# Small triangle products of the first third of the tokens: odd chunks in the other column half of the array, two PSUM tiles instead of one

## The chip, the cores and the metric

The kernel runs on one core of one Trainium2 chip. The metric is device time in microseconds (us) of one execution. A core has five engines that run side by side: TensorE (PE in the profile; PEld is its weight load), VectorE (DVE), ScalarE (ACT), GpSimd (POOL) and SyncE (SP), which here issues nearly all DMA transfers. Each engine works through its own instructions strictly in the order in which they stand, and waits on semaphores for the others.

## The reference

One layer of a bidirectional diffusion backbone over 128 context tokens and 2048 latent tokens, 1024 channels, fp32. All tokens are normalised and modulated, and go through one input projection; half of the channels (8 heads of 64) then run an RWKV-7 recurrence in both directions, the other half a gated short convolution; one output projection and a normalisation end it.

```python
def step(S, inp):
    r_t, w_t, k_t, v_t, kk_t, a_t = inp
    s_kk = jnp.einsum('bdhij,bdhj->bdhi', S, kk_t)
    S = (S * w_t[..., None, :] - s_kk[..., :, None] * (kk_t * a_t)[..., None, :]
         + v_t[..., :, None] * k_t[..., None, :])
    return S, jnp.einsum('bdhij,bdhj->bdhi', S, r_t)
```

The kernel does not step through tokens one by one. It cuts them into 34 chunks of 64. For each chunk, head and direction it needs a 64x64 product of two scaled operands, called alpha and beta below; of these products the triangles by the diagonal and the low off-diagonal block are kept in DRAM (scratch arrays `at` and `lo`), and a later stage solves with them. Those 64x64 products are what the change touches.

## The kernel before, in words

The work is written as a program of tiles; a scheduler then puts the instructions of each engine in an order, by a model of its own of how long each takes, and that order is fixed when the kernel runs. The trace's line numbers are those of the source.

**Stages.** Phase 1 computes the projections, the gates, the convolution and the scaled operands. It goes over the tokens in three thirds (`THIRD`: blocks 0 and 1, 2 and 3, 4 and 5; a block is 384 tokens, six chunks, the last 256). Within a third it goes over four groups `g` of 128 channels (two heads each), and for each group over the two blocks `j` of the third: `mixA` (the operands of the recurrence and the triangle products), `convB`, then `gateA`, `gateB`. Phase 2 solves, carries the states and forms the outputs; phase 3 is the output projection.

**The dense work around.** Each projection is 24 matmuls of 128x128 by 384 columns (L166 to L168; tiles `mmk`, `mmr`, `mmc`, `mmu`, `mmv`, `mmg`, `mmgb`, `mmb`). `lup` adds two matmuls (L420, L421) into a tile `up` of the same pool of five PSUM tiles (`pmm`). A smaller pool, `pax`, has three PSUM tiles with the tag `ax`, used in turn by `part_sum` (L210, L211: tiles `pss`, `psb`, `psq`), by the triangle products (`psA`) and by a transpose (`psv`). Whoever takes the next `ax` tile waits until the last reader of the tile three takings back is done.

**The triangle products.** `mixA` makes, for each direction `d`, the operands (`pair`, VectorE, L443 to L455; the last of them is L455) and calls `triangles`. In the first third (`late` is empty) it calls it once for each direction, 16 calls in all; in the second and third third once for both directions together (`todo` holds two). A call does six chunks times two heads of 64x64 by 64 columns. Head `h` takes the array's row half `h`. `place(d, h)` chooses the column half, and with it the half of the PSUM partitions that the result goes to: direction 0 puts head 0 in the upper and head 1 in the lower half, direction 1 the other way. So a call for one direction uses two of the four 64x64 quarters of the array, and a call for both directions all four, with one PSUM tile for each direction.

**After the products.** ScalarE copies the PSUM tile into the tile `ta` (L382, 128 x 384) and then two strips of 32 partitions over it (L384, two copies of 32 x 192). SyncE stores both halves of `ta` to DRAM: `at` (L385, pieces of 32 numbers) and `lo` (L386, per partition 6 x 32 numbers in a row). `ta` has two buffers; before the products it held an activation (L439), which VectorE reads for L454. So L439 of a later call waits until the stores of an earlier call have landed.

**Other names used below.** `wr` and `w` are weights on their way in (L130 load, L131 and L132 split, L133 store of the split); `wgate`/`psgr` a side product spread over the first third (L196); `t` is L426 (ScalarE's reading of `up`); `ct` L516; `sqx`/`ssq` the norm of the next third's tokens; `ops` the stored operands (L356).

## Time and profile before

| what | value |
|---|---|
| time, median of 3 runs | 1651.73 us (1645.61, 1651.73, 1653.22) |
| profiled execution: span, first to last instruction | 1642.5 us (its own time outside the span is not on the page) |
| mean granted TensorE clock | 0.974 |
| first triangle product | at 97.57 us of the span |
| last of the first third's 16 calls | at 371.08 us |
| first call of the second third | at 424.14 us |

The page names an engine's busy time, then groups of instructions by source line with their count, and for idle time the instruction that ended it. A row of the timeline gives start, duration, engine, line and tile, and in brackets how long the engine had been idle and what released it; successive equal instructions are merged into one row. A matmul of fp32 numbers stands as two records, so twelve 64x64 products are 24 records.

### The profile page before, as it was taken

Reading aid. Unit: us, or ns where it says so; the run is one execution under the profiler, and the core shown is the slowest. Engines: PE = TensorE matmul, PEld = TensorE weight load, DVE = VectorE, ACT = ScalarE, POOL = GpSimd, SP = SyncE. Lnnn points to the kernel's source line nnn. Section 1 sums busy time; section 2 is a strip of 40 time slices with the busy share of each in tenths; the row PEclk is TensorE's granted clock in tenths of the full one; section 3 lists DMA queues with packets and bytes.
Section 4 is the critical chain, followed back from the end, with each engine's and each line's share of the span. In section 5 each row is a group of like instructions: output and inputs, shape, how many; then the busy total and the mean of one; then the engine's idle time right before and its main releaser. Section 6 shows DMA issues by size and latency. Waiting matters only on the chain.

```text
span 1642.5 us, 42385 instructions
## 1 busy us (share of the span) xinstructions
PE 1531.9 (93%) x17160; PEld 1405.2 (86%) x17160; DVE 1104.6 (67%) x2220; ACT 762.7 (46%) x1617; POOL 586.8 (36%) x1040
## 2 busy tenths in 40 slices
PE   5899999999999999999989999989999988789998
PEld 2899988999999999999988898878888876668886
DVE  5876978784738685658788794566776764574333
ACT  4554565554425452425554023757666673432222
POOL 0011211110112021102667474888888832022221
PEclk8899999999999999999999999999999998889999
DMA  9677668664746564656867858767767663264342
GB/s 377 202 272 251 237 222 300 212 230 179 236 156 195 176 210 149 203 182 203 275 203 228 285 173 256 183 166 188 215 169 202 185 160 93 66 199 166 122 151 93
DMA packets 237988, 327.23 MB, mean 199 GB/s; under 512 B 91288, under 2 KB 191896, under 8 KB 223712
## 3 DMA queue, kind: packets, MB, share of 16 engines
q1 hardware_dynamic: 231840, 318.55, 61.3%
q0 software_dynamic: 1200, 3.93, 0.6%
q8 instruction: 135, 2.21, 0.6%
q10 hardware_dynamic: 4752, 2.04, 0.5%
q14 instruction: 61, 0.50, 0.1%
HBM read 207.92 MB, written 116.54 MB: 198 GB/s over the span
## 4 chain that ended last, share of the span: by engine, by line
PE 45%; POOL 9%; DVE 8%; ACT 4%; issue 4%; DMA 3%; SPq 0%; DVEq 0%; POOLq 0%; ACTq 0%
POOL zt L950 4%; PE psu L1381 4%; PE psu L1382 4%; PE psu L1383 4%; POOL ztmp L947 3%; PE psE L840 2%; PE psS L840 2%; ACT fg L829 1%; PE mmc L166 1%; PE mmg L168 1%; PE mmg L166 1%; PE mmg L167 1%; PE mmc L167 1%; PE mmc L168 1%; PE mmv L166 1%
## 5 line engine op out<-in xcount | busy, mean ns | idle before, releaser
L950 POOL TENSOR_TENSOR zt<-zt,ztmp 128x30 f32<-128x30 f32 (+7 forms) x390 | 153.0, 392 | 30.6
L840 PE MATMUL psE<-fg 128*64 128x128 f32 x2176 | 135.4, 277 | 15.8 <-ACT fg L831 13.6
L840 PEld LDWEIGHTS psE<-fg 128*64 128x64 f32 x2176 | 120.6, 139 | 22.4 <-ACT fg L831 15.6
L840 PE MATMUL psS<-sv,E 128*64 128x64 f32 x2176 | 98.6, 233 | 19.0 <-DVE sv L1147 18.5
L840 PEld LDWEIGHTS psS<-sv,E 128*64 128x64 f32 x2176 | 81.6, 143 | 34.8 <-DVE sv L1147 24.9
L329 POOL TENSOR_TENSOR shk<-rawl 128x384 f32<-128x384 f32 (+1 forms) x24 | 23.5, 979 | 241.1 <-ACT rawl L325 221.8
L829 ACT ACTIVATE fg<-psX 64x512 f32<-64x512 f32 x136 | 80.5, 592 | 37.3 <-PE psX L840 35.2
L1448 POOL TENSOR_TENSOR z<-z,x 128x512 f32<-128x512 f32 x32 | 41.8, 1307 | 137.9 <-DVE z L1444 114.4
L947 POOL TENSOR_TENSOR ztmp<-ab,zt 128x60 f32<-128x60 f32 (+4 forms) x165 | 85.9, 521 | 12.9
L1147 DVE TENSOR_TENSOR sv<-psS,pc 64x128 f32<-64x128 f32 x254 | 63.8, 278 | 39.5 <-PE psS L840 37.6
L329 POOL TENSOR_TENSOR shv<-rawl 128x384 f32<-128x384 f32 (+1 forms) x24 | 21.3, 888 | 165.0 <-ACT rawl L325 164.8
L831 ACT COPY fg<-psG 64x256 f32<-64x256 f32 x136 | 49.9, 367 | 52.5 <-DVE fg L1048 29.0
L1048 DVE TENSOR_TENSOR fg<-psG,consts 64x256 f32<-64x256 f32 x136 | 57.4, 422 | 25.1 <-ACT fg L831 11.2
L1041 DVE TENSOR_TENSOR F<-psF,consts 128x512 f32<-128x512 f32 x68 | 44.1, 681 | 44.5 <-PE psF L840 44.5
L446 POOL COPY pcs<-pp 128x6 f32<-128x6 f32 (+1 forms) x48 | 20.9, 435 | 139.0 <-ACT pp L435 135.1
L166 PE MATMUL mmc<-h,w 128*128 128x384 f32 (+1 forms) x192 | 64.6, 336 | 5.9 <-ACT q1r L327 4.1
L1109 DVE TENSOR_TENSOR E<-psE,consts 128x256 f32<-128x256 f32 x136 | 53.2, 418 | 21.3 <-PE psE L840 19.9
L166 PE MATMUL mmg<-h,w 128*128 128x384 f32 (+1 forms) x192 | 63.6, 331 | 3.8 <-ACT q1v L327 3.8
L831 ACT COPY E<-psE 128x256 f32<-128x256 f32 x136 | 48.5, 373 | 36.8 <-DVE E L1109 27.4
L166 PE MATMUL mmb<-h,w 128*128 128x384 f32 (+1 forms) x192 | 63.3, 329 | 1.5 <-ACT ta L439 1.5
L166 PE MATMUL mmgb<-h,w 128*128 128x384 f32 (+1 forms) x192 | 64.0, 333 | 0.4 <-ACT q1r L327 0.4
L166 PE MATMUL mmv<-h,w 128*128 128x384 f32 (+1 forms) x192 | 63.4, 330 | 0.3 <-ACT q1r L327 0.3
(325 smaller groups left out, 5169.9 us busy)
## 6 DMA issues: line engine op xcount, KB each, us to landing
w<-scr_wsp SPq DMA_DIRECT2D x68, 1024.0 KB, 5.7
scr_wsp<-w SPq DMA_DIRECT2D x34, 1024.0 KB, 4.9
scr_ops<-pair SPq DMA_DIRECT2D x80, 384.0 KB, 4.5
wr<-in_win SPq DMA_DIRECT2D x34, 512.0 KB, 6.8
o<-scr_ops SPq DMA_DIRECT2D x32, 512.0 KB, 6.0
fg<-scr_ops SPq DMA_DIRECT2D x120, 128.0 KB, 3.6
x<-in_x SPq DMA_DIRECT2D x17, 512.0 KB, 8.5
wadas<-in_wada SPq DMA_DIRECT2D x8, 1024.0 KB, 13.5
```

Source lines behind the costliest of these rows:

```text
L166: T.matmul(ps[:, :n], w[:, 0, k], hh[:, 0, k, :n], start=k == 0, stop=False)
L829: P.activation(dst, src, AF.Copy, scale=-1.0)
L831: P.copy(dst, src)
L840: r = T.matmul(*a, start=True, stop=True, **k)
L947: eng.tensor_tensor(tv, ab[:, j:j + 2, j + 2:32].unsqueeze(1).broadcast_to((128, kn, 2, n)), zt[:, :kn, j:j + 2].unsqueeze(3).broadcast_to ...
L950: last = eng.tensor_tensor(zt[:, :kn, j + 2:32], zt[:, :kn, j + 2:32], tv[:, :, r], ALU.subtract).ins
L1048: V.tensor_tensor(g.gs[H[1 - h], g.op, h, us], ps[gi][r, :, 64:128], B.mG[r, g.d].unsqueeze(1).broadcast_to((64, 4, 64)), ALU.mult)
L1109: V.tensor_tensor(to(H[1]), of(H[1]), B.mE[:, g.d].unsqueeze(1).broadcast_to((128, 4, 64)), ALU.mult)
L1147: r = V.tensor_tensor(dst, sp[gi][0:64, q], B.pc[0:64, d, 2 * p:2 * p + 2, c:c + 1].broadcast_to((64, 2, 64)), ALU.mult)
L1381: T.matmul(ps[:], mh[:, n], hi[:, cs], start=start and n == 0, stop=False)
L1382: T.matmul(ps[:], mh[:, n], lo[:, cs], start=False, stop=False)
L1383: T.matmul(ps[:], ml[:, n], hi[:, cs], start=False, stop=stop and n == 3)
```

## The change

Only calls with one direction, those of the first third, are changed: `split` is 2 there and 1 elsewhere. A call now takes two PSUM tiles of `pax`, one for even and one for odd chunks. Odd chunks (`k` = 1) use `place(d, 1 - h)`, the other column half, so their result stands with the halves of the partitions swapped. ScalarE copies each tile into the chunks of `ta` that it holds (L388, every second chunk; four strips at L390 instead of two). The stores of the even chunks go out as before but for every second chunk (L392 `at`, L393 `lo`); those of the odd chunks need two DMAs each, one for each half of the partitions, which puts the halves back in place (L397 `at`, L398 `lo`). So a call has 2 + 4 copies instead of 1 + 2, and 6 stores instead of 2; every stored row is now in pieces of 32 numbers.

```diff
-        ps = [pax.tile([128, 6, 64], F32, tag="ax", name=f"psA{g}_{j}_{x[0]}") for x in todo]
+        split = 3 - len(todo)
+        m = nch // split
+        ps = [[pax.tile([128, 6 // split, 64], F32, tag="ax", name=f"psA{g}_{j}_{x[0]}_{k}") for k in range(split)] for x in todo]
         for u in range(nch):
             us = slice(u * 64, u * 64 + 64)
+            k = u % split
             for h in range(2):
                 r = slice(h * 64, h * 64 + 64)
                 for p_, (d, al, be, _) in zip(ps, todo):
                     x, y = (be, al) if d == 0 else (al, be)
-                    T.matmul(p_[place(d, h), u, :], x[r, us], y[r, us], start=True, stop=True)
+                    T.matmul(p_[k][place(d, h ^ k), u // split, :], x[r, us], y[r, us], start=True, stop=True)
         for p_, (d, _, _, t_) in zip(ps, todo):
             o = t_[:, :].rearrange("p (k u i) -> p k u i", k=2, i=32)
-            P.copy(o[:, :, :nch], p_[:, :nch].rearrange("p u (k i) -> p k u i", k=2))
-            for r in (slice(32, 64), slice(96, 128)):
-                K.mark = P.copy(o[r, 0, :nch], p_[r, :nch, 32:64]).ins
-            nc.sync.dma_start(S["at"][d, g, c0:c0 + nch].rearrange("u s b j i -> (s b j) u i"), o[:, 0, :nch])
-            nc.sync.dma_start(S["lo"][d, g * 128:g * 128 + 128, c0:c0 + nch], o[:, 1, :nch])
+            at, low = S["at"][d, g, c0:c0 + nch], S["lo"][d, g * 128:g * 128 + 128, c0:c0 + nch]
+            for k in range(split):
+                q = slice(k, nch, split)
+                P.copy(o[:, :, q], p_[k][:, :m].rearrange("p u (k i) -> p k u i", k=2))
+                for r in (slice(32, 64), slice(96, 128)):
+                    K.mark = P.copy(o[r, 0, q], p_[k][r, :m, 32:64]).ins
+                if k == 0:
+                    nc.sync.dma_start(at[q].rearrange("u s b j i -> (s b j) u i"), o[:, 0, q])
+                    nc.sync.dma_start(low[:, q], o[:, 1, q])
+                else:
+                    for x in range(2):
+                        rx, ry = slice(x * 64, x * 64 + 64), slice(64 - x * 64, 128 - x * 64)
+                        nc.sync.dma_start(at[q, x].rearrange("u b j i -> (b j) u i"), o[ry, 0, q])
+                        nc.sync.dma_start(low[rx, q], o[ry, 1, q])
```

The matmul stands at L379 before and at L382 after; lines behind the function are 12 higher after (L420 before is L432 after, L426 is L438, L439 is L451). The scheduler makes a new order of the first third out of this; from the second third on the engines' orders are the same but for the names.

TensorE, group 2, block 0, direction 0 (the call that starts at 259.10 us in the profile before). Before:

```order
L420 MATMUL up_211_2636<-lw_1_522,ups 128x384
L421 MATMUL up_211_2636<-lw_1_522,ups 128x384
L196 MATMUL psgr_2066<-wgate_2759,scp 32x512
L379 MATMUL psA_0_0_2358<-pair_2345,pair_2353 64x64 x12
L196 MATMUL psgr_2066<-wgate_2759,scp 32x512
L420 MATMUL up_213_2645<-lw_1_524,ups 128x384
L421 MATMUL up_213_2645<-lw_1_524,ups 128x384
L166 MATMUL mmc_2699<-h_496,w_169_2236 128x384
```

And after, at the same place (the last number but one of `psA` is the direction's tile, 0 for even and 1 for odd chunks):

```order
L432 MATMUL up_211_2724<-lw_1_522,ups 128x384
L433 MATMUL up_211_2724<-lw_1_522,ups 128x384
L196 MATMUL psgr_2130<-wgate_2855,scp 32x512 x2
L382 MATMUL psA_0_0_0_2422<-pair_2409,pair_2417 64x64 x2
L382 MATMUL psA_0_0_1_2423<-pair_2409,pair_2417 64x64 x2
...
L432 MATMUL up_213_2733<-lw_1_524,ups 128x384
L433 MATMUL up_213_2733<-lw_1_524,ups 128x384
L166 MATMUL mmc_2795<-h_496,w_169_2300 128x384
```

The products alternate between two PSUM tiles, and both halves of the side product `psgr` stand ahead of them instead of one.

ScalarE at the same place. Before (`ta_0_186` is the tile that takes the products, `t_1_207` the reading of an `up`):

```order
L225 ACTIVATE sqx_3_2510<-x_2432 128x384
L382 COPY ta_0_186_2343<-psA_0_0_2358 128x384
L384 COPY ta_0_186_2343<-psA_0_0_2358 32x192 x2
L408 ACTIVATE kk_1_201_2556<-ok_2543,vec 128x384
L402 ACTIVATE sq_1_200_2545<-ok_2543,vec 128x384
L426 ACTIVATE t_1_207_2594<-up_206_2591,dv 128x384
L426 ACTIVATE t_1_212_2639<-up_211_2636,dv 128x384
```

And after:

```order
L388 COPY ta_0_186_2407<-psA_0_0_0_2422 128x6x32
L388 COPY ta_0_186_2407<-psA_0_0_1_2423 128x6x32
L390 COPY ta_0_186_2407<-psA_0_0_0_2422 32x3x32 x2
L225 ACTIVATE sqx_3_2590<-x_2512 128x384
L390 COPY ta_0_186_2407<-psA_0_0_1_2423 32x3x32 x2
L420 ACTIVATE kk_1_201_2636<-ok_2623,vec 128x384
L414 ACTIVATE sq_1_200_2625<-ok_2623,vec 128x384
L438 ACTIVATE t_1_207_2674<-up_206_2671,dv 128x384
L438 ACTIVATE t_1_212_2727<-up_211_2724,dv 128x384
```

Between the products and the first `t` there now stand six copies and the `sqx` step instead of three copies.

SyncE's queue, at the first call. Before:

```order
L356 DMA scr_ops_57<-pair_662 128x2x384
L386 DMA scr_lo<-ta_0_30_652 128x192
L356 DMA scr_ops_58<-pair_699 128x2x384
L385 DMA scr_at<-ta_0_30_652 128x6x32
L133 DMA scr_wsp<-w_65_1054 128x2048
L130 DMA wr_70_1067<-in_win 128x1024
```

And after:

```order
L356 DMA scr_ops_57<-pair_662 128x2x384
L393 DMA scr_lo<-ta_0_30_652 128x3x32
L392 DMA scr_at<-ta_0_30_652 128x3x32
L397 DMA scr_at<-ta_0_30_652 64x3x32
L398 DMA scr_lo<-ta_0_30_652 64x3x32
L397 DMA scr_at<-ta_0_30_652 64x3x32
L398 DMA scr_lo<-ta_0_30_652 64x3x32
L356 DMA scr_ops_58<-pair_707 128x2x384
L133 DMA scr_wsp<-w_65_1086 128x2048
L130 DMA wr_70_1099<-in_win 128x1024
```

Six stores in a row stand ahead of the second operand store and of the weights' store and load, where before there were two.

## The prediction

> **What bounds the kernel now.** I read the page first, for the busiest engine, then only the stretch in which the change lies: the windows by engine, TensorE's waits there, and the products' own records.
>
> ```profile
> span 1642.5 us, 42385 instructions
> PE 1531.9 (93%) x17160; PEld 1405.2 (86%) x17160; DVE 1104.6 (67%) x2220; ACT 762.7 (46%) x1617; POOL 586.8 (36%) x1040
> ```
>
> The 16 changed calls lie between 85 and 380 us. The next two answers are that window, with busy us of PE, PEld, DVE, ACT and POOL, the granted clock and the DMA engines' share, and TensorE's waits in it.
>
> ```profile
> 85.00:380.00 295.00, 291.43 (x1925) 273.04 (x1925) 231.66 (x399) 155.70 (x303) 48.91 (x54) 1.00 0.71 241
> PE mmc L166 <- ACT t L426: 1.8, 1, 1.8
> PE mmu L166 <- ACT ct L516: 0.6, 1, 0.6
> PE up L420 <- ACT rawc L332: 0.5, 1, 0.5
> PE up L420 <- ACT t L426: 0.4, 1, 0.4
> PE pss L210 <- ACT hshs L202: 0.3, 1, 0.3
> ```
>
> TensorE works 291.43 of 295.00 us at the full clock, and its 3.6 us of pauses are the five waits shown, all on ScalarE. VectorE has 63 us to spare, ScalarE 139. So in this stretch a microsecond less on TensorE is a microsecond earlier, as long as no other engine makes it wait; and what follows in the second third stands in the same order as before, so it moves as a whole.
>
> **What the products cost.** TensorE's time on L379 alone, in the stretch with one direction to a call and in the one with both:
>
> ```profile
> 85.00:380.00 295.00, 14.63 (x384) 12.44 (x384) 1.00 0.71 241
> 400.00:690.00 290.00, 7.48 (x384) 6.38 (x384) 1.00 0.58 186
> ```
>
> The same 384 records take 14.63 us in 16 calls on two quarters of the array and 7.48 us in 8 calls on four. Single calls of the timeline, one of the first third, one of the second, and one of the third with four chunks:
>
> ```profile
> 110.26 0.92 PE L379 MATMUL psA<-pair,pair 64*64 64x64 f32 x24
> 446.99 0.93 PE L379 MATMUL psA<-pair,pair 64*64 64x64 f32 x48
> 760.80 0.69 PE L379 MATMUL psA<-pair,pair 64*64 64x64 f32 x32
> ```
>
> On four quarters, 16 records more cost 0.93 - 0.69 = 0.24 us, so 0.015 us a record; 24 records then take 0.69 - 8 x 0.015 = 0.57 us instead of 0.92. The changed call walks the four quarters in another order (both rows of one PSUM tile, then both of the other) than a call with two directions (one row into both tiles, then the other); each quarter still comes once in four products, so I take the same pace. That removes 0.35 us a call, **16 x 0.35 = 5.6 us** on the path. The bounds are no gain, if the other order doesn't overlap, and 14.63 - 7.48 = 7.2 us, if the start of a call cost nothing.
>
> **ScalarE's copies.** Durations by shape, the third's last blocks against the others:
>
> ```profile
> L384 ACT COPY stages<-psA x32: 257/286/313, 750.2 to 901.9; 32x192 f32<-32x192 f32 x16, 32x128 f32<-32x128 f32 x16
> L382 ACT COPY ta<-psA x16: 459/479/503, 98.5 to 374.4; 128x384 f32<-128x384 f32 x16
> L382 ACT COPY stages<-psA x16: 351/420/522, 748.6 to 899.8; 128x384 f32<-128x384 f32 x8, 128x256 f32<-128x256 f32 x8
> ```
>
> 64 columns fewer save 56 ns on the strip (313 to 257, the ends of that row), 128 fewer 128 ns on the wide copy (479 to 351). So 32x96 is about 230 ns, 128x192 about 290 ns. A call goes from 479 + 2 x 313 = 1105 ns to 2 x 290 + 4 x 230 = 1500 ns: 0.40 us more, 6.4 us in all, beside 139 us of idle ScalarE. It costs nothing except where TensorE waits for ScalarE.
>
> The longest of TensorE's waits is such a place. TensorE and then ScalarE there:
>
> ```profile
> 258.13 1.05 PE L196 MATMUL psgr<-wgate,scp 128*32 128x512 f32 x2
> 259.10 0.92 PE L379 MATMUL psA<-pair,pair 64*64 64x64 f32 x24
> 259.95 1.05 PE L196 MATMUL psgr<-wgate,scp 128*32 128x512 f32 x2
> 260.92 0.44 PE L420 MATMUL up<-lw,ups 128*128 128x384 f32 x1
> 263.34 0.44 PE L166 MATMUL mmc<-h,w 128*128 128x384 f32 x1 [1.79 <-ACT t L426]
> 266.86 0.92 PE L379 MATMUL psA<-pair,pair 64*64 64x64 f32 x24
> ...
> 259.21 0.52 ACT L225 ACTIVATE sqx<-x 128x384 f32<-128x384 f32 x1 [1.05 <-DVE ssq L226]
> 260.06 0.48 ACT L382 COPY ta<-psA 128x384 f32<-128x384 f32 x1 [0.33 <-PE psA L379]
> 260.58 0.64 ACT L384 COPY ta<-psA 32x192 f32<-32x192 f32 x2
> 261.24 0.61 ACT L408 ACTIVATE kk<-ok,vec 128x384 f32<-128x384 f32 x1
> 262.07 0.61 ACT L402 ACTIVATE sq<-ok,vec 128x384 f32<-128x384 f32 x1 [0.21 <-DVE pair L454]
> 262.71 0.58 ACT L426 ACTIVATE t<-up,dv 128x384 f32<-128x384 f32 x1
> ```
>
> The copies begin when the products end, and `mmc` begins when the first `t` behind them is done (262.71 + 0.58). By the order shown, the second half of `psgr` (0.97 us, 259.95 to 260.92) now runs ahead of the products, and `sqx` (0.52) and 0.40 of copies come between them and `t`. New: products at 258.13 + 2 x 0.97 = 260.07, over at 260.64, then 1.50 copies, 0.52 `sqx`, 0.61 + 0.21 + 0.61 + 0.58: 264.7 against 263.34. This call loses 1.4 us where the sum above has it gain 0.35, so **1.75 us come back**. It could be nothing if ScalarE does `sqx` sooner, or 2.2 if `sqx` waits for VectorE again.
>
> **PSUM tiles.** A call takes two of three `ax` tiles, so the second direction's odd tile waits for the copies of the first direction's even tile, and `psb` right behind it for the odd one's. In the stretch above 6.9 us lie between the end of the one direction's products and the start of the other's (259.95 to 266.86). Copies of about 2 us, started at the end of the products, are done by then. I take nothing for it, with half a microsecond a call as the other end.
>
> **Stores.** SyncE issues six DMAs a call instead of two. The issue, the landing and who waits for `ta`:
>
> ```profile
> L386 SPq DMA_DIRECT2D scr_lo<-ta x16: 319/324/885, 99.0 to 374.9; - x16
> L385 SPq DMA_DIRECT2D scr_at<-ta x16: 359/440/1655, 100.1 to 376.3; - x16
>   DMA scr_at<-ta: 8.5, 3
> DMA to landing us min/median/max: 1.6/4.3/5.6
> scr_lo<-ta SPq DMA_DIRECT2D x16, 96.0 KB, 4.6
> scr_at<-ta SPq DMA_DIRECT2D x16, 96.0 KB, 2.0
> ```
>
> Four more at 0.32 to 0.44 us are 1.6 us more in the queue, in which the next operand store, weights' store and weights' load stand behind them; with the copies, `ta` is free 2.0 us later. The `lo` rows go from 768 bytes to 128-byte pieces; `at` goes out in such pieces already and lands in 2.0 us against 4.6, so I see no price for small pieces here, in a stretch where the DMA engines are at 0.71. The Trainium skill (DMA: Bandwidth & Descriptors, Specifications) puts line rate at pieces of 512 bytes and more, which speaks against this change; these two landing times do not bear it out at this size. By the page the `lo` stores would land later than their 4.6 us, which is the slower rival below; by the rows the sum stays as it is.
>
> Three times before, L439 waits for such a store, 8.5 us in all. The longest, and TensorE in the four microseconds that lie within it:
>
> ```profile
> 277.60 0.58 ACT L439 ACTIVATE ta<-up,dv 128x384 f32<-128x384 f32 x1 [5.04 <-DMA scr_at<-ta]
> 274.00:278.00 4.00, 4.00 (x25) 4.00 (x24) 3.59 (x5) 0.40 (x1) 0.00 (x0) 1.00 1.10 395
> ```
>
> TensorE didn't notice: 4.00 of 4.00 busy. What hides it is the lead of the operands: a late `ta` makes a late L455, and the products wait for that. The least lead of the 16 calls and the greatest (its products are the 259.10 above):
>
> ```profile
> 340.17 0.54 DVE L455 TENSOR_TENSOR pair<-pair,t 128x384 f32<-128x384 f32 x1
> 342.21 0.92 PE L379 MATMUL psA<-pair,pair 64*64 64x64 f32 x24
> 253.67 0.55 DVE L455 TENSOR_TENSOR pair<-pair,t 128x384 f32<-128x384 f32 x1
> ```
>
> Leads of 342.21 - 340.71 = 1.5 us and 259.10 - 254.22 = 4.9 us stand against 2.0 us of lateness: only the thinnest shows, by 0.5. I take **1.0 us** for all, two such calls; the ends are nothing and 16 x 0.5 = 8.
>
> **The sum.** -5.6 + 1.75 + 1.0 = -2.85 us, 0.17% of the median. The page gives the profiled execution's span alone, 1642.5; the median of the runs is 9.2 us above it, and I leave that as it is: the span would be 1639.6, the time 1651.73 - 2.85 = **1648.9 us**. Half a per cent, 8.3 us, is about what a measurement of this kernel can tell from no change (its three runs span 7.6), so the gain as worked out would not be told apart.
>
> **The rivals.**
> *All of it is given back.* The new order puts other work ahead of the products, and ScalarE, on which all five waits hang, has more to do just ahead of what TensorE waits for. If four places lose 1.4 us like the one above, or the 16 calls 0.35 each, the time is 1651.7. For it: TensorE had no slack to ScalarE in five places. Against: 139 us idle on ScalarE, and a 5.04 us stall that cost nothing.
> *The quarters don't overlap.* If two rows into one PSUM tile in succession hold each other up, nothing is gained and the 2.75 us of costs remain: 1654.5. Against: the calls with two directions use the same four quarters and two tiles at 0.015 us a record.
> *Slower: the copies and stores take the lead away.* If the last of six stores lands as late as the slowest before (5.6 instead of 2.0 us), `ta` is 2.0 + 3.6 = 5.6 us late. Against a middle lead of 3.2 that is 2.4 us of stopped TensorE a call, 38 us in 16, net 1651.7 + 33 = 1684. It turns slower by half a per cent once a call loses (5.6 + 8.3)/16 = 0.87 us. Against: the longest wait for such a store fell into a stretch with the DMA engines at 1.10, and even there TensorE went on. The Trainium skill (TensorEngine Tiling (Array Packing), PSUM Bottleneck) warns of the same end, that tiling speeds up TensorE but not the emptying of PSUM; here the copies of a call do grow from 1.1 to 1.5 us while its products shrink to 0.57.
> *Faster than that.* If the new order also does away with the old 3.6 us of pauses: 1651.7 - 5.6 - 3.6 = 1642.5, 0.56% faster.
>
> **How the numbers follow.** The forecast 0.52, all given back 0.22, no overlap 0.06, slower 0.12, faster 0.08. The first three lie within half a per cent, 0.80 together. The range goes from the faster case, 1642.5, past no overlap at 1654.5 to 1656.5, which takes in 2 us more of stops; of the slower case nearly all is left out, and half of the faster one. The price of that is under 2 in 10.
>
> **What would show it.** Right: the L382 rows of the first third at 0.57 us for 24 records, their TensorE time in 85 to 380 at about 9.1 us (x384); TensorE's wait of `mmc` for `t` grown from 1.8 to over 3 us; and the first call of the second third, at 424.14 before, at about 421.3.
>
> ```profile
> 424.14 0.94 PE L379 MATMUL psA<-pair,pair 64*64 64x64 f32 x48
> ```
>
> Wrong: records at the old pace; `psA`, `psb` or `pss` waiting for copies (the PSUM tiles), `psA` waiting for `pair` (the stores); or a first third that ends earlier while the rest takes that back.

## The result, and the profile after

The changed kernel takes 1657.53 us (median of 10 runs, 1652.91 to 1668.75), the kernel before 1650.65 (10 runs, 1645.61 to 1653.37) beside it: a ratio of 1.0061, 95% interval 1.0043 to 1.0078. The change makes the kernel slower by about 0.6%, where 1648.9 was forecast; 1657.5 also lies just beyond the range. The profiled execution took 1656.89 us, its span is this:

```profile
span 1655.1 us, 42533 instructions
PE 1530.7 (92%) x17160; PEld 1402.0 (85%) x17160; DVE 1104.6 (67%) x2220; ACT 769.0 (46%) x1665; POOL 585.8 (35%) x1040
```

TensorE is busy 1.2 us less than before over a span that is 12.6 us longer, so what came is idle time, or time at a lower clock, not work. (This time is 1.8 us more than its span. By that, an estimate, the execution profiled before took 1644 us, less than any of the ten times above; so 12.6 us is more than what the change costs, 6.9 us by the medians.) The products first: TensorE's time on L382 alone in the stretch of the first third, one call, and the first call of the second third.

```profile
85.00:380.00 295.00, 8.67 (x360) 6.61 (x360) 0.98 0.71 234
```

```profile
266.85 0.58 PE L382 MATMUL psA<-pair,pair 64*64 64x64 f32 x24
...
432.49 0.94 PE L382 MATMUL psA<-pair,pair 64*64 64x64 f32 x48
```

A call takes 0.58 us where 0.57 was forecast (0.92 before): the four quarters run side by side. The copies have nearly the forecast sizes, 0.32 and 0.23 us where 0.29 and 0.23 were worked out, so a call's copies grow by 0.46 us and not by 0.40:

```profile
L388 ACT COPY ta<-psA x30: 298/320/351, 97.7 to 375.5; 128x192 f32<-128x192 f32 x30
L390 ACT COPY ta<-psA x60: 230/232/233, 98.3 to 376.6; 32x96 f32<-32x96 f32 x60
```

And yet the first call of the second third starts at 432.49 instead of 424.14, 8.35 us late in place of 2.85 early. The window of all engines and TensorE's waits in it say why:

```profile
85.00:380.00 295.00, 281.14 (x1853) 262.83 (x1854) 225.96 (x385) 155.41 (x337) 48.22 (x53) 0.98 0.71 234
```

```profile
PE up L432 <- ACT t L438: 5.0, 1, 5.0
PE mmc L166 <- ACT t L438: 5.0, 3, 3.4
PE mmc L166 <- ACT q1r L327: 1.6, 1, 1.6
PE mmu L166 <- ACT ct L528: 0.7, 1, 0.7
PE psA L382 <- DVE pair L467: 0.7, 1, 0.7
PE mmc L166 <- ACT rawc L332: 0.5, 1, 0.5
```

TensorE is busy 281.14 of 295 us, before it was 291.43. The waits add up to 13.5 us against 3.6, nearly all on ScalarE again, and three of them are new or grown: `up` for `t`, 5.0 us, which was 0.4; `mmc` for `t`, 3.4 us, which was 1.8; and `mmc` for `q1r`, 1.6 us at 178.6, which isn't among the waits of that window before. The first two are followed here. The granted clock of the window has gone from 1.00 to 0.98. Where, is seen in narrow windows behind the two pauses (columns as before, the clock is the third from the end), and in the rows of the matmuls at the first:

```profile
243.00:248.00 5.00, 5.00 (x18) 5.00 (x19) 4.63 (x11) 4.41 (x10) 0.52 (x1) 0.56 1.01 389
...
271.00:275.00 4.00, 3.66 (x12) 3.66 (x13) 3.61 (x5) 3.20 (x7) 0.95 (x2) 0.57 1.06 323
275.00:280.00 5.00, 5.00 (x51) 4.68 (x50) 2.00 (x5) 4.61 (x14) 1.13 (x2) 1.00 0.72 211
```

```profile
242.78 0.69 PE L432 MATMUL up<-lw,ups 128*128 128x384 f32 x1 [5.04 <-ACT t L438]
...
243.59 0.52 PE L166 MATMUL mmc<-h,w 128*128 128x384 f32 x1
243.91 0.52 PE L167 MATMUL mmc<-h,w 128*128 128x384 f32 x1
...
247.60 0.34 PE L167 MATMUL mmc<-h,w 128*128 128x384 f32 x1
247.78 0.34 PE L168 MATMUL mmc<-h,w 128*128 128x384 f32 x1
```

Behind each of the two pauses TensorE has half its clock for some microseconds, and the last window has the full clock again: a matmul every 0.32 us at 243.6, every 0.18 at 247.6. So a pause is paid twice.

The reason for the longer one stands in ScalarE's timeline. First the kernel before, then the one after; `h` are the eight steps of making h2, `t` is what `up` waits for.

```profile
227.79 4.32 ACT L155 ACTIVATE h<-x,sh 128x384 fp32r<-128x384 f32 x8 [1.97 <-DVE x L154]
...
237.36 0.58 ACT L426 ACTIVATE t<-up,dv 128x384 f32<-128x384 f32 x1
```

```profile
235.51 1.11 ACT L155 ACTIVATE h<-x,sh 128x384 fp32r<-128x384 f32 x2
...
237.48 2.12 ACT L155 ACTIVATE h<-x,sh 128x384 fp32r<-128x384 f32 x4
...
240.24 0.60 ACT L155 ACTIVATE h<-x,sh 128x384 fp32r<-128x384 f32 x1
240.86 1.28 ACT L438 ACT_TABLE_LOAD   x1
242.15 0.58 ACT L438 ACTIVATE t<-up,dv 128x384 f32<-128x384 f32 x1
```

Before, the eight steps were over at 232.1, ahead of the readings of `mmk`. After, seven of them run between 235.5 and 240.8, right ahead of `t`, with a table load of 1.28 us behind them. What made them late is found by going back through what they need, before and after: the transposes `psv` of V, the tile `vt` that VectorE makes from them, the low part `hslq` of the norm sum of block 2, its product `psq`, and the scaling of x (L154).

```profile
211.44 0.49 PE L482 MATMUL psv<-idt,ov 128*128 128x128 f32 x3
213.91 0.42 DVE L492 SCALAR_TENSOR_TENSOR vt<-vmean,psv 128x256 f32<-128x256 f32 x1
217.92 1.01 POOL L203 TENSOR_TENSOR hslq<-ssq,hshq 128x384 fp32r<-128x384 f32 x1 [2.83 <-DVE bsum L503]
220.79 0.34 PE L211 MATMUL psq<-hslq,onf 128*128 128x384 f32 x1
227.15 4.32 DVE L154 SCALAR_TENSOR_TENSOR x<-x,gs,ssq 128x384 f32<-128x384 f32 x8
```

```profile
215.20 0.49 PE L494 MATMUL psv<-idt,ov 128*128 128x128 f32 x3
220.04 0.41 DVE L504 SCALAR_TENSOR_TENSOR vt<-vmean,psv 128x256 f32<-128x256 f32 x1
226.63 1.93 POOL L203 TENSOR_TENSOR hslq<-ssq,hshq 128x384 fp32r<-128x384 f32 x1 [11.45 <-ACT w L131]
228.62 0.44 PE L211 MATMUL psq<-hslq,onf 128*128 128x384 f32 x1
232.32 4.68 DVE L154 SCALAR_TENSOR_TENSOR x<-x,gs,ssq 128x384 f32<-128x384 f32 x8
```

`psv` takes an `ax` tile of PSUM, as `psA` does, which now takes two of three; it comes 3.8 us later. `vt` and `hslq` share one buffer (both have the tag `vt`), so `hslq` waits until `vt` is stored. On the way the delay grows: `vt` is made 6.1 us later; its store is now issued behind a store and a load of weights (L133 and L130, at 218.82 and 219.21) that came after it before, and has landed at 226.10 instead of 217.32. So `hslq` is 8.7 us later. (The bracket at `hslq` names `w`, which ended at about the same time. The semaphores name the store: in the kernels before and after, e3, e4 and e8, `hslq` starts 0.5 to 0.6 us behind its last landing.) `psq`, the scaling and the h2 steps follow. None of these instructions is one that the change touches.

### The profile page after: what moved, and what is told of

It is laid out like the page before. It is cut to its first block, busy times and chain, and to the rows that moved or that the text cites. A ratio compares the mean times of both kernels' runs of the same rounds, so it can differ in the third digit from the quotient of the medians.

```text
span 1655.1 us, 42533 instructions
## 1 busy us (share of the span) xinstructions
PE 1530.7 (92%) x17160; PEld 1402.0 (85%) x17160; DVE 1104.6 (67%) x2220; ACT 769.0 (46%) x1665; POOL 585.8 (35%) x1040
## 3 DMA queue, kind: packets, MB, share of 16 engines
q8 instruction: 135, 2.21, 0.6%
## 4 chain that ended last, share of the span: by engine, by line
PE 46%; DVE 9%; ACT 5%; POOL 5%; DMA 4%; issue 4%; SPq 1%; DVEq 0%; ACTq 0%; POOLq 0%
PE psu L1393 4%; PE psu L1394 4%; PE psu L1395 4%; PE psE L852 3%; PE psS L852 2%; ACT fg L841 2%; POOL zt L962 2%; PE psX L852 1%; POOL ztmp L959 1%; PE psG L852 1%; PE mmc L166 1%; PE mmu L168 1%; PE mmu L167 1%; PE mmu L166 1%; PE mmv L166 1%
## 5 line engine op out<-in xcount | busy, mean ns | idle before, releaser
L852 PEld LDWEIGHTS psE<-fg 128*64 128x64 f32 x2176 | 121.2, 139 | 19.6 <-ACT fg L843 13.5
L166 PE MATMUL mmc<-h,w 128*128 128x384 f32 (+1 forms) x192 | 65.6, 342 | 11.3 <-ACT q1r L327 5.7
L843 ACT COPY E<-psE 128x256 f32<-128x256 f32 x136 | 48.7, 373 | 37.5 <-DVE E L1121 27.9
L167 PE MATMUL mmc<-h,w 128*128 128x384 f32 (+1 forms) x192 | 64.2, 334 | 0.0
```

The costliest lines, as they stand in the source:

```text
L166: T.matmul(ps[:, :n], w[:, 0, k], hh[:, 0, k, :n], start=k == 0, stop=False)
L167: T.matmul(ps[:, :n], w[:, 0, k], hh[:, 1, k, :n], start=False, stop=False)
L843: P.copy(dst, src)
L852: r = T.matmul(*a, start=True, stop=True, **k)
```

## The experiments

**Theory A**, formed from this: the change's own operations are as cheap as forecast, but with them the instructions come in another order; the h2 steps stand late and in front of `t`, TensorE pauses, and half clock follows the pauses. **Theory B**: the added copies or stores cost the time themselves, by load. **Theory C**: any change of the order costs some microseconds somewhere, and this is one throw of the dice. Each run, of 4 to 12 executions, is timed beside runs of the kernel before on the same chip, so the ratios are compared, not the medians.

One table holds the first third of every profile, where the changed calls lie. What follows it takes 1216.5 to 1230.7 us in the 18 profiles (1218.4 before); that part is taken up at e2 and e14 alone. "First third" is the time from the first call of the products (97.57 in before) to the first call of the second third (424.14). "Pauses" is the sum of the gaps of over 0.25 us between TensorE's matmuls in it. "Half clock" is the time in it with a granted clock of 0.5, and in brackets how much of that lies outside the pauses. "Rest" is the first third less the pauses and less half of the time in brackets, so the work at the full clock: after, 335.4 - 12.8 - 8.0/2 = 318.5 (before rounding).

| run | quarters side by side | first third | pauses (longest) | half clock | rest | ratio to before, 95% interval |
|---|---|---|---|---|---|---|
| before | no | 326.6 | 3.6 (1.80) | 0 | 323.0 | |
| after | yes | 335.4 | 12.8 (5.04) | 10.2 (8.0) | 318.5 | 1.0061 (1.0043 to 1.0078) |
| e1 | yes | 325.1 | 7.8 (2.21) | 0 | 317.3 | 1.0014 (0.9993 to 1.0036) |
| e2 | no | 329.4 | 4.6 (2.87) | 6.8 (6.2) | 321.7 | 0.9965 (0.9950 to 0.9979) |
| e3 | no | 339.4 | 11.3 (4.28) | 10.2 (9.6) | 323.3 | 1.0071 (1.0050 to 1.0093) |
| e4 | yes | 338.1 | 16.2 (8.88) | 13.7 (9.6) | 317.1 | 1.0028 (1.0014 to 1.0043) |
| e5 | no | 341.9 | 13.7 (7.75) | 20.5 (12.8) | 321.8 | 1.0079 (1.0053 to 1.0105) |
| e6 | yes | 329.5 | 8.6 (3.03) | 10.2 (9.4) | 316.1 | 1.0001 (0.9981 to 1.0020) |
| e7 | no | 332.1 | 6.8 (2.99) | 6.8 (6.1) | 322.3 | 1.0024 (1.0004 to 1.0044) |
| e8 | yes | 334.7 | 12.0 (4.32) | 10.2 (9.5) | 318.0 | 1.0049 (1.0029 to 1.0070) |
| e9 | yes | 345.5 | 19.0 (4.97) | 17.1 (15.5) | 318.8 | 1.0177 (1.0154 to 1.0200) |
| e10 | yes | 329.0 | 9.7 (2.31) | 3.4 (3.1) | 317.7 | 1.0071 (1.0046 to 1.0095) |
| e11 | no | 330.2 | 6.3 (2.25) | 3.4 (3.4) | 322.2 | 1.0067 (1.0046 to 1.0088) |
| e12 | yes | 324.5 | 6.0 (2.91) | 3.4 (3.4) | 316.8 | 1.0015 (1.0001 to 1.0030) |
| e13 | yes | 324.3 | 7.3 (2.91) | 0 | 317.0 | 0.9980 (0.9961 to 0.9998) |
| e14 | no | 326.6 | 4.5 (2.87) | 0 | 322.1 | 0.9957 (0.9935 to 0.9979) |
| e15 | no | 328.9 | 6.0 (1.49) | 0 | 322.9 | 1.0009 (0.9993 to 1.0025) |
| e16 | yes | 325.8 | 8.3 (2.09) | 0 | 317.5 | 1.0001 (0.9981 to 1.0020) |

The rest is 316.1 to 318.8 us in the ten profiles with the quarters side by side and 321.7 to 323.3 in the eight without (means 317.5 and 322.4). That is 4.9 us of work less, whatever else a kernel does; all that differs besides is pauses and half clock.

**e1: the link cut in the kernel after.** The low part of the norm sum gets a place of its own, so it no longer waits for `vt`:

```diff
-        lo = ta_.tile([128, 384], F32R, tag="vt", name=f"hsl{nm}", bufs=1)
+        lo = lo or ta_.tile([128, 384], F32R, tag="vt", name=f"hsl{nm}", bufs=1)
...
-        ps = part_sum(onf, acc, n, f"q{j}", eng)
+        if j == 2:
+            hs[2] = hl.tile([128, 2, 8, 384], F32R, tag="h", name="h2")
+        ps = part_sum(onf, acc, n, f"q{j}", eng, hs[2][:, 1, 7] if j == 2 else None)
```

> The kernel after, with one buffer more: the low part of the norm sum of block 2 (hslq2, POOL at L203) no longer takes the buffer of vt1_0 but the last eighth of h2, which is free until h2 is made. Nothing is left out. Theory A (the second PSUM tile of the triangles puts the transposes psv1_0 later, and through vt1_0's buffer, hslq2, psq2 and the eight h2 steps of ScalarE it makes t_2_0 late, so that TensorE pauses 5.04 us at 242.78 and runs 6.8 us at half clock behind it): the eight h2 steps stand ahead of the readings of mmk again, the pause at up0 falls from 5.04 to under 1 us, the half clock there (about 3.4 us of loss) goes, the first call of the second third starts about 8 us earlier than the 432.5 us of the kernel after, and the time is about 1649.5 (1647 to 1652). Theory B (the added copies of ScalarE and the four more stores cost it themselves, by load): the start stays at 432.5 and the time at 1657.5, within 1.5. Theory C (any new order costs some us somewhere): the pause moves to another place, and the time stays over 1654.

Its rows at the place, in time's order: the second product of `psq` (its operand now lies in `h`), the scaling, the h2 steps, `t`, and the first call of the second third. Then what is left of the wait.

```profile
216.64 0.34 PE L211 MATMUL psq<-h,onf 128*128 128x384 f32 x1
223.53 3.79 DVE L154 SCALAR_TENSOR_TENSOR x<-x,gs,ssq 128x384 f32<-128x384 f32 x7
226.72 4.15 ACT L155 ACTIVATE h<-x,sh 128x384 fp32r<-128x384 f32 x8
239.16 0.57 ACT L440 ACTIVATE t<-up,dv 128x384 f32<-128x384 f32 x1
...
423.14 0.94 PE L384 MATMUL psA<-pair,pair 64*64 64x64 f32 x48
```

```profile
PE mmc L166 <- ACT t L440: 3.2, 3, 1.6
PE up L434 <- ACT t L440: 2.2, 1, 2.2
```

The h2 steps are 8.8 us earlier and in one piece, the pause is 2.2 us in place of 5.0, the other pause 1.6 in place of 3.4, and there is no half clock. The first third is 10.2 us shorter with the same products, copies and stores, and the ratio falls from 1.0061 to 1.0014. Theory A's size for the start is met (9.4 us earlier, where about 8 was expected). The time by the ratio is 1653.0, one microsecond above its range. The pause is 2.2 and not under 1 us: a cast of a weight (`w`, L131, 1.04 us from 237.73) stands in front of `t` there. Theory B falls as the main cause in the first third. e16 is the same kernel once more, below.

**e2: the same buffer in the kernel before.** The same edit in the kernel before, triangles as they were.

> The kernel before with the same one buffer more for the low part of the norm sum of block 2; the triangles as before. Nothing is left out. Theory A: before has a pause of only 0.42 us at up0, so there is little to win: 1650.6, within 1.5 us, first call of the second third at 424 within 2. Theory C (any new order costs some us): slower by 3 us or more. If it is faster by several us, then the buffer is worth something without the triangles' change, and the gain of the other run isn't the change's loss undone.

Neither theory's number came. The kernel is faster by 0.35%, though its first third isn't shorter (it has a pause of 2.87 us with 6.8 us of half clock behind it). The expectation asked whether e1's gain is then the change's loss undone. The traces speak for it: behind the first third ScalarE, VectorE and GpSimd have the order of the kernel before in after, e8, e1 and e16 (but for two instructions of VectorE in e1 and e16), and another one in e2 and e14, and e1 isn't shorter there than after (1230.7 us against 1222.6). So what e1 wins over after lies in the first third, and what e2 wins does not. But with the buffer in both, the kernel with the change (1.0014, and 1.0001 in e16) is still slower than the one without (0.9965, and 0.9957 in e14). How much of that is the other order of the last part no run tells. e14 takes it up again.

**e3: two tiles, six copies, six stores, but no quarters.**

```diff
-                    T.matmul(p_[k][place(d, h ^ k), u // split, :], x[r, us], y[r, us], start=True, stop=True)
+                    T.matmul(p_[k][place(d, h), u // split, :], x[r, us], y[r, us], start=True, stop=True)
...
-                        rx, ry = slice(x * 64, x * 64 + 64), slice(64 - x * 64, 128 - x * 64)
+                        rx = ry = slice(x * 64, x * 64 + 64)
```

> The kernel after with odd chunks in the same column half as even ones (two PSUM tiles, six copies and six stores per call stay; the stores no longer swap halves). The quarters of the two row halves then follow each other as in the kernel before. Nothing is left out. Theory A: the pauses and their half clock stay (the order of the instructions is the same), and the 16 calls lose the 0.35 us each that the quarters gained: 1657.5 + 5.6 = 1663, between 1661 and 1666, first call of the second third at 437 to 439. Rival (the quicker triangles only wait longer for the operands, so their gain never reached the end): 1657.5 within 1.5. If the array doesn't run the quarters side by side at all, it is 1657.5 too, with 24 records in 0.92 us in both.

The pauses and the half clock stay as in the kernel after (4.28 and 3.29 us), so they don't come from the pace of the products. The first third is 4.0 to 4.7 us longer than in the two profiles of the kernel after, between the two expectations: the work is 4.8 to 5.3 us more, and the pauses take 0.7 to 1.5 of it back. The whole time (1.0071) can't be told from that of the kernel after.

**e4: the halves swapped back in the copies, two stores.**

```diff
+                if k == 0:
+                    P.copy(o[:, :, q], src)
+                else:
+                    for x in range(2):
+                        P.copy(o[x * 64:x * 64 + 64, :, q], src[64 - x * 64:128 - x * 64])
...
+            nc.sync.dma_start(at.rearrange("u s b j i -> (s b j) u i"), o[:, 0, :nch])
+            nc.sync.dma_start(low, o[:, 1, :nch])
```

> The kernel after, but the halves are swapped back in ScalarE's copies (seven per call in place of six) and each call has two stores as before in place of six. Nothing is left out. Its order differs from that of the kernel after in the first third; the second product of psq2 comes after 14 of the 24 products of mmk, and four h2 steps still run between the readings of mmk and t_2_0. Theory A: the pause at up0 stays at 4 us or more, and the time at 1655 to 1660. Theory B, stores' side (the four more stores per call make SP and the buffers late): 64 stores fewer bring it back to 1649 to 1651. Theory B, copies' side: over 1658, since there is one copy more.

The pauses are the greatest so far, but not where Theory A had them: 1.72 us at `up` and 1.79 at the `mmc` behind it, 8.88 us at the next block's `mmc`. The first third is longer than after, and still the whole is at 1.0028, the low end of what Theory A gave and above that of the stores' side. What it wins lies in the last part; see e14. For the stores alone it says little, because its order differs too.

**e5: the pause without the change.** Triangles, copies and stores as before; the end of the norm and the h2 steps are only written one block later.

```diff
-                if ga:
+                slow = t3 == 0 and ga == 1 and h
+                if ga and not slow:
                     next(more, None)
...
-                if ga:
+                for _ in range(4 * (j == js[1]) if slow else 1 if ga else 0):
                     next(more, None)
```

> The kernel before, triangles unchanged; only the end of the norm of block 2 and the making of h2 are written one block later in the program, so that in ScalarE's order four to six of the eight h2 steps stand between the readings of mmk and t_2_0, as in the kernel after. Nothing is left out. Its order in the last part is that of the runs e2 and e4 (the first products of psF15 behind 22 of psa5's matmuls in place of 8), which took 50.5 and 47.4 us from psF14 to psF16's place where before took 58.6. Theory A (late h2 steps make t_2_0 late, TensorE pauses, half clock follows): without any change of the triangles a pause of 4 us or more comes at up0 or at the mmc behind it, with 3.4 us or more of half clock, and the first call of the second third starts 6 to 13 us later than the 424.1 us of the kernel before; the gain of some 8 us in the last part stands against it, so the time is 1647 to 1655. Rival (the triangles' own operations are what makes the first third long): the start stays within 2 us of 424, and the time is about 1643.

TensorE's wait, the clock behind the pause at 241 and around the one at 267, and ScalarE's h2 steps with `t`:

```profile
PE mmc L166 <- ACT t L426: 10.8, 3, 7.7
```

```profile
243.00:248.00 5.00, 5.00 (x19) 5.00 (x18) 5.00 (x12) 4.44 (x9) 0.48 (x1) 0.57 1.01 334
266.00:275.00 9.00, 1.25 (x26) 1.11 (x24) 5.47 (x11) 4.71 (x10) 0.44 (x1) 0.60 0.95 378
```

```profile
236.43 1.68 ACT L155 ACTIVATE h<-x,sh 128x384 fp32r<-128x384 f32 x3 [0.51 <-DVE x L154]
...
240.83 0.58 ACT L426 ACTIVATE t<-up,dv 128x384 f32<-128x384 f32 x1
```

With not one instruction of the triangles changed, the first third is 341.9 us, 15.3 longer than before, and the ratio 1.0079: the late h2 steps are enough to lose more in the first third than the change lost there. The longest pause came at an `mmc`, 7.75 us, which the expectation allowed, but two parts of it were wrong. The second third starts 15.9 us later, not 6 to 13; and the 8 us that the last part was to give back didn't come (744.3 us from the last call to the end, before 744.8; the order there isn't that of e2 and e4, see e14).

**e6 and e7: the two ways of storing, with h2 early.** e6 is e4 and e1 together. e7 is e2 with the two stores of a call split into six:

```diff
+            for k in range(split):
+                q = slice(k, nch, split)
+                if k == 0:
+                    nc.sync.dma_start(at[q].rearrange("u s b j i -> (s b j) u i"), o[:, 0, q])
+                    nc.sync.dma_start(low[:, q], o[:, 1, q])
+                else:
+                    for x in range(2):
+                        rx = slice(x * 64, x * 64 + 64)
+                        nc.sync.dma_start(at[q, x].rearrange("u b j i -> (b j) u i"), o[rx, 0, q])
+                        nc.sync.dma_start(low[rx, q], o[rx, 1, q])
```

> The kernel after with both edits: halves swapped back by ScalarE's copies (seven copies and two stores per call), and the low part of the norm sum of block 2 in h2's place. Nothing is left out. All eight h2 steps are ahead of the readings of mmk and t_2_0 stands right behind those, and the last part has the order of e2, so it differs from e2 in the triangles alone. Theory A (without the late h2 steps the quarters bring their 5.6 us less a part that the next waits take back): the first call of the second third starts 1 to 5 us before that of e2 (426.9 us with 6.8 us of half clock, so 423.5 without), and the time is 1638 to 1643 beside e2's 1642.7. Theory B (the copies themselves cost: 112 copies in place of 48 in the first third): 1646 or more.

> The kernel of e2 (before, norm low part in h2's place) with each call's two stores of the first third split into six, as in the kernel after, without swapped halves; the triangles and the copies as before. Nothing is left out. ScalarE's order at t_2_0 and the last part are those of e2. Theory A (the stores lie beside other work): the same as e2, 1642.7 within 2 us, ratio 0.9965 within 0.0012, and the first call of the second third at 423 to 427. Theory B, stores' side: 3 us or more over e2.

e6 has the work of the quarters (316.1) but a pause of 3.03 us, where `psA` waits for `pair`, and 10.2 us of half clock, and ends where e2 ends in the first third. Its ratio, 1.0001, is on Theory B's side of the expected times; the profile shows no more than the pauses for it, and the last part hasn't e2's order, as was expected. e7 went against Theory A and as the stores' side had it: 1.0024 where 0.9965 was expected. Its work is as without six stores (322.3 against 321.7 and 322.1), its pauses are 2.2 us more than e2's, and its first third 2.7 us longer than e2's and 5.5 longer than e14's. Its longest pause, 2.99 us, stands where e2 has its 2.87, but at `psA`, which waits for `pair`; that `pair` ends a row of VectorE's work from 262.65 on, in which nothing waits for a store. So the six stores don't come off free in that kernel, but its order isn't e2's either, in the first third or in the last part (59.5 us in the stretch shown at e14, e2 50.5). What they cost to the whole stays open.

One thing e7 settles: it has six stores and one PSUM tile, and its `psv` stands 0.2 us behind the product `psb`, at 215.16. So it does in all six profiles with one tile; in all twelve with two it stands 3.3 to 4.0 us behind `psb`, in e4 and e6 too, which have two stores. So it is the second tile, with its copies, and not the stores, that goes with the late `psv`.

**e8: the kernel after once more.**

> The kernel after, unchanged, for a second profile of it on the chip of these runs. Both theories: ratio 1.006 within 0.002; a pause of 4 to 6 us at up0 near 240 us and of 3 to 4 us at mmc near 270 us, 6 to 14 us of half clock in the first third, and the first call of the second third at 430 to 435 us. If the pauses don't come back, they are of one execution and theory A falls.

All of it came: pauses of 4.32 and 3.37 us, 10.2 us of half clock, the second third at 431.25, ratio 1.0049.

**e9 to e12: strips on GpSimd.** The strips come from the wide copy's result instead of PSUM:

```diff
-                    K.mark = P.copy(o[r, 0, q], p_[k][r, :m, 32:64]).ins
+                    K.mark = G.tensor_copy(o[r, 0, q], o[r, 1, q]).ins
```

e9 is the kernel after with this, e10 has e1's buffer besides, e11 is the kernel before with this, e12 is e6 with this.

> The kernel after with the strip copies taken off ScalarE: GpSimd copies the two 32-row strips from the wide copy's result in SBUF (o[r, 1] to o[r, 0]), in all calls of all thirds. Nothing is left out. ScalarE's order at t_2_0 is that of the kernel after (the eight h2 steps between the readings of mmk and t_2_0). Theory A: the two pauses stay (4 to 5 us at up0, 3 to 4 us at mmc), with 6 to 14 us of half clock, and the first third (first call to first call of the second third) is 333 to 336 us as in the kernel after (335.4, 334.7); ratio 1.003 to 1.007. Theory B, copies' side (64 strip copies of 0.23 us, 14.7 us of ScalarE in the first third, are what it costs): the pauses fall by half or more, the first third is 322 to 328 us, ratio under 1.001.

> The kernel of e9 with the low part of the norm sum of block 2 in h2's place, as in e1. Nothing is left out. All h2 steps are ahead of the readings of mmk; the cast of w26 still stands ahead of t_2_0. Theory A: no pause over 2.5 us, no half clock from 100 to 420 us, first third 321 to 326 us (e1: 325.1), ratio 0.996 to 1.0015. Theory C (each new order has its own pauses): first third over 328.

> The kernel before with the strip copies on GpSimd as in e9; triangles, stores and order at t_2_0 as before. Nothing is left out. Theory A: the kernel before has little to win there: first third 324 to 327.5 us (before 326.6), ratio 0.998 to 1.001. Theory B, copies' side: 3 us or more faster in the first third.

> The kernel of e6 (halves swapped back in the copies, two stores per call, norm low part in h2's place) with the strips on GpSimd: three ScalarE copies per call in place of seven. Nothing is left out. t_2_0 stands right behind the readings of mmk. Theory A: work without pauses and half clock of 315 to 317 us in the first third (as in the five profiles with quarters), pauses of 5 to 8 us in all, first third 320 to 326 us; ratio 0.995 to 1.000, the version that beats both if any of these does. Theory C: a pause of 3 us or more comes somewhere, with half clock behind it, and the first third is 327 or more, as in e6 (329.5).

TensorE's longest wait in e9, and GpSimd's new copies there:

```profile
PE up L432 <- ACT t L438: 5.0, 1, 5.0
```

```profile
L390 POOL COPY ta<-ta 32x96 f32<-32x96 f32 x64 | 31.8, 496 | 43.5 <-ACT ta L388 28.7 <-DVE t L439 5.9 <-DMA scr_mixT<-ob 4.4
```

With the strips gone from ScalarE the pause at `up` is still 5.0 us and the one at `mmc` 2.9, since the h2 steps are where they were: Theory B's side of the copies falls. The first third is ten microseconds longer than Theory A had it, with further pauses of 2.36 and 1.7 us from 328 us on. A strip takes 496 ns on GpSimd against 232 on ScalarE, and the versions with it are slow, e11 by 0.7% with no other change and a first third of 330.2 where 324 to 327.5 was expected. In e10 the longest pause falls to 2.31 us as Theory A had it, but the first third is 329.0, which was Theory C's side, and the ratio 1.0071; both are worse than Theory A expected. e12 has the first third that was expected, 324.5, but the whole is at 1.0015, above the expected range.

**e13 to e16: what is left of the change when h2 is early.** e13 has the strips on GpSimd in the first third alone, e14 is e2 once more, e15 is e1 with e3's edit, e16 is e1 once more.

```diff
+                    K.mark = (P.copy(o[r, 0, q], p_[k][y * 64 + 32:y * 64 + 64, :m, 32:64]) if late else G.tensor_copy(o[r, 0, q], o[r, 1, q])).ins
```

> The kernel of e12 with the strips on GpSimd in the first third alone; in the later thirds ScalarE copies them as in the kernel before. Nothing is left out. Theory A: first third 320 to 326 us as in e12 (324.5), the rest as in the kernel before, ratio 0.996 to 1.000. If e12's rest was long by chance and not by the strips on GpSimd, it is the same as e12, 1.0015 within 0.0015.

> The kernel of e2 (before, norm low part in h2's place) once more, unchanged. If its gain is real: ratio 0.995 to 0.998. If it was chance: 0.999 to 1.002. By its pauses (4.6 us in all in e2's profile, 4.3 in the kernel before) it should be the same as the kernel before, and what half clock it has in the first third (6.8 us there) can come or not.

> The kernel of e1 with odd chunks in the same column half as even ones (as e3 is to the kernel after): the quarters of the two row halves follow each other; six stores, no swapped halves. Nothing is left out. The order on ScalarE and GpSimd is that of e1. Theory A (the quarters are worth 5.6 us less what the next wait takes back, 1 to 3 us): 2.5 to 5.6 us more than e16 in the first third, between 327 and 331 us without half clock, and 2 to 6 us more in the time. Rival (the gain is taken back wholly by the waits for t): the same first third as e16 within 1 us, with pauses shorter by 5 us.

> The kernel of e1 (after, norm low part in h2's place) once more, unchanged, on the chip of e14 and e15. Theory A: first third 324 to 327 us, no pause over 2.5 us, ratio 0.999 to 1.003, so 4 to 10 us less than the kernel after's 1.0061 and 1.0049.

e15 and e16 differ in the column half alone. Their products in the first third, e15's first, and their waits of `up` for `t`:

```profile
85.00:380.00 295.00, 14.63 (x384) 12.44 (x384) 1.00 0.72 238
```

```profile
85.00:380.00 295.00, 9.25 (x384) 7.05 (x384) 1.00 0.72 238
```

```profile
PE up L434 <- ACT t L440: 2.1, 1, 2.1
```

The same 384 records take 5.38 us less in e16. Its first third is 3.1 us shorter (325.8 against 328.9), its pauses 2.4 us longer, as Theory A had it: nearly half of the gain is taken back, because a TensorE that arrives sooner waits longer for the same work of ScalarE (1.1 us of the 2.4 are for `t`, where e15 waits 4.2 us in all and e16 5.3). On the whole time 1.0001 and 1.0009 can't be told apart. e16 also confirms e1.

e14 confirms e2: 0.9957. Its first third is that of the kernel before, to 0.1 us. Where its profile differs most is the last part, in the stretch from 1342 to 1401 us before, which is 1351 to 1399 in e14:

```profile
1342.20:1400.80 58.60, 48.52 (x854) 40.18 (x852) 27.18 (x66) 26.39 (x55) 14.82 (x19) 0.88 0.46 123
```

```profile
1350.70:1399.40 48.70, 45.10 (x858) 38.16 (x855) 28.01 (x67) 26.36 (x55) 13.95 (x19) 0.96 0.51 135
```

The same stretch takes 48.7 in place of 58.6 us: TensorE idles 3.6 us in it, not 10.1, and has more of its clock. Not all of it is won: e14 comes to that stretch 6.6 us later behind the last call of the products, so it wins 4.0 us from there to the end (740.8 against 744.8). The order of the instructions differs there too, in a place that the edit doesn't touch. In e2, e4 and e14, which have the same order on ScalarE, VectorE, GpSimd and SyncE, SyncE issues a load `woraw` ahead of each of two rows of eight loads `fg`; in the kernel before and in e5, e6 and e7 the second `woraw` stands within a row, behind its third load. The stretch takes 50.5, 47.4 and 48.7 us in the first three and 55.4, 55.6 and 59.5 in e5, e6 and e7. So the order of the loads goes with the short stretch; no run changes it alone.

e13 came as expected, 324.3 us and 0.998. It is the fastest version with the change and ahead of both kernels; e14, without the change, is ahead of it by the ratio, though their intervals overlap.

## Why the prediction was wrong, step by step

- **The products, -5.6: right.** 0.58 us a call for 0.57; 14.63 us of records became 9.25 (e16), and the work without pauses is 4.9 us less in the mean of 18 profiles. The rival that the quarters don't overlap is out.
- **The copies, 0.40 us a call beside other work: nearly right in size, right in place.** They took 0.46 us a call more. Taking the strips off ScalarE (e9) left the pause at `up` as it was, 5.0 us, and the one at `mmc` at 2.9 in place of 3.4.
- **The wait of `mmc` for `t` at 259 to 263, +1.75: right for the wait, too large for the place.** The wait grew from 1.79 to 3.37 us, and from the end of the products to `mmc` it went as worked out, through copies and `sqx`: 3.9 us for 4.06 (before 3.3). But the two halves of `psgr` take 0.99 us when they run in a row, not 2 x 0.97, so from the start of `psgr` to `mmc` the place lost 0.3 us (5.48 against 5.21) and not 1.4. In e1 `sqx` is ahead of the copies, and the wait is 1.6 us, near the end that the prediction gave with "if ScalarE does `sqx` sooner".
- **The stores, +1.0: not settled.** In the profile after, TensorE waits 0.7 us for `pair`, once. The landing is what the rows forecast:

```profile
scr_lo<-ta SPq DMA_DIRECT2D x16, 48.0 KB, 3.1
scr_lo<-ta SPq DMA_DIRECT2D x32, 24.0 KB, 2.2
```

  The `lo` stores, now in pieces of 128 bytes and with a half and a quarter of the bytes, land in 3.1 and 2.2 us, where 768-byte pieces took 4.6. The slower rival, which had late stores stop TensorE in all 16 calls, is out. The Trainium skill's 512 bytes for line rate (DMA: Bandwidth & Descriptors, Specifications) don't show at this size. e15 gives a size for copies and stores together, as far as two orders can be compared: it has six of each and two tiles, but no quarters and no late h2 steps, and its first third is 2.3 us longer than before (forecast 1.75 + 1.0), its ratio 1.0009. e7's first third is 2.7 to 5.5 us longer than those of e2 and e14, in an order of its own.
- **The PSUM tiles, "I take nothing for it": the step that failed.** I asked only who waits for the copies of a tile, and for that nothing was right: neither `psA` nor `psb` waits for them. What I didn't ask is which other instructions take a tile of the same three. `psv` does; it was put later, and behind it, through a buffer that its copy `vt` shares with the norm, the h2 steps were put in front of `t`: 3.8 us late at `psv`, 8.7 at `hslq`, and a pause of 5.04 us where there was one of 0.4. That they, with the buffer, make the loss of the first third is shown by e1 and e16 (cut the link: 9 to 10 us of the first third come back) and by e5 (late h2 steps alone: 15.3 us lost). With the link cut the first third is 0.8 to 1.5 us shorter than before, on the side that the prediction had with its 2.85. That the second tile puts `psv` late is shown only by its place in the two-tile and one-tile kernels; a kernel with more `ax` tiles wasn't tried.
- **What follows a pause: left out of the sum.** 10.2 us at half clock in the first third, 8.0 of them outside the pauses, cost 4.0 us. The account of the profile after: -4.5 of work, +9.3 of pauses, +4.0 of clock (before rounding), 8.8 in all by the table (326.6 to 335.4).
- **The rivals.** "All of it is given back" named the mechanism, other work ahead of what TensorE waits for on ScalarE, and priced it at the gain; pauses and clock took 13.3 us, more than twice that. I had spread it over many small places and not followed one chain to its end. The 139 us of idle ScalarE that I held against it are a mean: from 235.5 to 246 ScalarE has no gap. Theory C is neither shown nor out: e2 and e14 move by -0.35 and -0.43% with an edit of one buffer that leaves the first third as long as it was or longer, so an edit of this kernel can move the time by near half a per cent for reasons that it wasn't made for.

## What to carry to other kernels

Before pricing a change that takes one more tile of a pool, list who else takes tiles of that pool and who shares a buffer with those, and follow each of them to the engine that the bottleneck waits for; the order after the change shows it, if one reads the whole block and not only the changed calls. A gain on the busiest engine is worth its work less what the next wait takes back: here 5.4 us of matmul time became 3.1 us of the first third even with the late h2 steps gone (e15 and e16). And in this kernel a pause of TensorE of 3 us or more is to be priced with the clock behind it: one of 2.99 us in e7 brought 6.8 us of half clock, 3.1 us of time, so about twice its length.

## What the runs showed of the hardware

Half clock comes in steps of 3.41 us and follows pauses. All eleven pauses of 2.99 us and more in the first thirds of the 18 profiles (2.99 to 8.88 us) had 3.4 to 10.2 us of half clock at or behind them. Of the nine between 2.2 and 2.92 us, five had it and four had not; the same kernel shows both (e2 and e14, 2.87 us each, 6.8 us and none). The Trainium skill (TensorE: Matmul & The Clock Gate, What's actually happening) has a free-running window of 3413 ns and half rate after an idle one. The steps agree with that; but pauses shorter than a window are enough here, down to 2.31 us in e10. In e6 and e11 half clock even came behind single pauses of 1.84 and 1.78 us, and in e4, e5 and e9 behind two shorter ones close together. With a window that runs freely it would depend on how the pause falls, which may be why one kernel shows both; no run here tests that.
